# A planner that knows which neighbours cannot overlap, and a fixed table of seeds for its order

## The chip, the cores and the metric

The program runs on one core of one Trainium2 chip. Its time is the device time of one execution in microseconds, from the host's single launch to the end of the outputs; lower is better. Of each kernel several executions are timed, and one more is taken with the hardware profiler.

## What is computed

One inference step of a decoder trunk of two layers, for a prompt of 512 tokens and a group of 8 x 8 sample tokens, which share all weights (576 tokens together, 1024 channels, all in 32-bit floats).

```
h = rms_norm(x);  m = pooling mixer (layer 0) or gated DeltaNet mixer (layer 1)
x = x + rms_norm(m)
h = rms_norm(x);  f = (silu(h @ w_gate) * (h @ w_up)) @ w_out
x = x + rms_norm(f)
```

The pooling mixer takes trailing means over 2, 4, 8 and 16 positions, minus the token, and a linear map in each of four groups. The gated DeltaNet mixer projects h to q, k, v and z, runs a short causal convolution of width 4, and then a chunked delta rule over 16 value heads of 128 x 128: in each chunk a unit lower triangular matrix is inverted, and a state S is carried from chunk to chunk (the scan). Outputs are the tokens, the pooling rows, the convolution rows and the states.

## The kernel before

A matrix product in 32 bits is made of three TensorE products in the rounded type `fp32r`: every weight and every activation is split into a high part (`wh`, `hH`, `aH`; a ScalarE copy) and a low part (`wl`, `hL`, `aL`; the difference, on VectorE or GpSimd), and `mm3` multiplies high by high, high by low and low by high. The work comes in these stages: the pooling mixer, the first feed-forward (partly with Strassen's products), the DeltaNet mixer in four groups of four value heads, its output product, and the second feed-forward. In the DeltaNet mixer the group's own work (the *core*: decay matrices `QD`, the inverse built in `ii` and `Uw`, the small sample problem with `BD`, `TQ` and `ks`, then the scan with `vn`, `ve` and `S`, and the sample states `St`) is a chain in which TensorE, ScalarE and VectorE take turns, and the projections of the next group (`ps_m`, three products for each of eight blocks of rows) are there to fill TensorE in the meantime.

In what order each engine gets its instructions is not written in the code. The class `Plan` records every operation with the tiles that it reads and writes, gives each a cost (`cost`: a time `t`, and a hold `t` minus 85 ns on VectorE or minus 102 ns on ScalarE, since an instruction may start before its forerunner's end), and at `finish` lists them: `forward` goes through time, and each engine takes the operation of highest rank among those whose inputs are ready by these costs. Operations marked `EITHER` go to VectorE or GpSimd, whichever is taken first. The ranks are the latest starts that `backward` finds from an earlier list. On one engine the program then runs strictly in the order that stands in the list; between engines semaphores hold an instruction until its inputs are there, however long that takes on the chip. Where `forward` sees TensorE without work for more than 300 ns, `idle_until` puts small products of a matrix of ones into a free bank (`ps_w`, called fillers below), which keep the array busy and compute nothing.

After 40 rounds over the whole list, `refined` goes over the list in windows of 60 us in steps of 30 us. In each window it tries up to 40 random shifts of the ranks (one shift for all operations that write the same tile), and keeps the one whose worst lateness is least; 16 passes of this are made, and a pass is kept where the listed end comes earlier. Its costs take no account of the partition at which an operand starts, nor of the steps of a GpSimd copy.

Of the kernel before, what the change touches and what calls it, by code (L numbers as in the profile page):

```python
# [16 lines left out]
PSUM = bass.MemoryType.PSUM  # L17
# [39 lines left out]
class Plan:  # L57
# [8 lines left out]

    LAT = {"PE": 55.0, "ACT": 36.0, "DVE": 36.0, "POOL": 70.0, "SP": 60.0}
# [8 lines left out]
    PASSES, SPAN, STEP, TRIES, FEW = 16, 60000.0, 30000.0, 40, 6  # L76
# [83 lines left out]
    def cost(self, eng, method, out, ins, k):  # L160
# [24 lines left out]
        if eng == "POOL":  # L185
            if method in ("memset", "tensor_copy"):
                t = 0.85 * n + (100 if method == "memset" else 183)
            elif method == "affine_select":
                t = 1.1 * n + 190
            else:  # L190
                bc = any(list(x.ap)[-1][0] == 0 for x in ins if self.size(x) > 1)
                t = (1.75 if bc else 2.2) * n + 180
            return t - 60, t
        if method == "transpose":
            flat = all(list(x.ap)[-1][0] == 1 for x in ins + [out])
            t = 1.27 * n + 50 if flat else 1.95 * n + 80
        elif method == "scalar_tensor_tensor":
            t = 1.04 * n + 210
        elif method == "reciprocal":
            t = 6.2 * n + 153  # L200
        elif method in ("tensor_copy", "tensor_scalar") and not ps:
            t = 0.58 * n + 160
        else:
            t = 1.04 * n + 160
        return t - 85, t

    def put(self, method, calls, a, k):
# [39 lines left out]
        if "PE" in calls:  # L247
            rows, cols = self.rows(ins[0]), list(outs[0].ap)[0][1]
            mode = rows + (1000 if "tile_position" in k and cols < 128 else 0)
            work = self.size(outs[0]) / 2.4 * (1 if ins[0].dtype != F32 else 2 if method == "transpose" else 4)  # L250
            work *= rows * min(1.0, 0.25 * -(-cols // 32)) / 128
        elif method == "activation":
            mode = self.TABLE.get(str(a[2]).split(".")[-1], 0)
        cost = {e: self.cost(e, method, outs[0], ins, k) for e in calls}
        two = method in ("tensor_tensor", "scalar_tensor_tensor", "tensor_scalar", "tensor_copy") \
            and not any(x.space == PSUM for x in ins)
        self.ops.append((calls, cost, a, k, sorted(preds), mode, work, next(iter(calls)), two, method,
                         {x.tensor.name for x in ins + outs if x.space == PSUM}))
# [13 lines left out]
    def finish(self):  # L272
# [48 lines left out]
    def refined(self, plan, draw):  # L321

        late = self.backward(plan[1], plan[2])
        rank = [-t for t in late]
        order = sorted(range(len(late)), key=late.__getitem__)
        names = [self.name(o) for o in self.ops]
        done, state, a, first = ([], []), None, 0.0, 0

        def behind(found, b):

            nonlocal first
            log, times, taken, busy = found[-2], found[-1], found[2], 0.0
            worst = max((t - late[i] for (i, e), (t, _) in zip(log, times) if e is not None), default=-1e12)
            while first < len(order) and state is not None and state[2][order[first]]:
                first += 1
            k = first
            while k < len(order) and taken[order[k]]:
                k += 1
            return worst if k == len(order) else max(worst, b - late[order[k]])

        while True:
            b = a + self.SPAN
            best = None
            tries = self.TRIES
            k = 0
            while k < tries:
                trial = rank
                if k:
                    off, by = {}, draw.choice(self.STIR[2:])
                    trial = rank[:]  # L350
                    for i in window:
                        off.setdefault(names[i], by * (2.0 * draw.random() - 1.0))
                        trial[i] += off[names[i]]
                found = self.forward(trial, state, b, late, best and best[0])
                k += 1
                if found is None:
                    continue
                value = behind(found, b)
                if k == 1:
                    window = [i for i, e in found[-2] if e is not None]  # L360
                    work = sum(self.ops[i][1]["PE"][0] for i, e in found[-2] if e == "PE")
                    if work > 0.995 * self.SPAN:
                        tries = self.FEW
                if best is None or value < best[0]:
                    best = value, trial
            rank = best[1]
            found = self.forward(rank, state, a + self.STEP)
            done[0].extend(found[-2])
            done[1].extend(found[-1])
            state, a = found[:-2], a + self.STEP  # L370
            if not found[0]:
                return max(found[3].values()), *done

# [54 lines left out]
    def forward(self, rank, state=None, until=None, due=None, limit=None):  # L428
# [4 lines left out]
        if state is None:  # L433
# [13 lines left out]
            quiet = {}  # L447
        else:
            todo, left, taken, free, ready, avail, when, mode, dma, port, phases, fast, recent, busy, turn, still, \
                quiet = state  # L450
            left, taken, when, recent = left[:], taken[:], when[:], recent.copy()
            free, mode, port, turn, still, quiet = (dict(v) for v in (free, mode, port, turn, still, quiet))
# [54 lines left out]
        while todo:  # L507
# [40 lines left out]
            if limit is not None and t - due[i] >= limit:  # L548
                return None
            if mine is not q:  # L550
                q.remove((-rank[i], i))
                heapq.heapify(q)
# [39 lines left out]
        return (todo, left, taken, free, ready, avail, when, mode, dma, port, phases, fast, recent, busy, turn, still,  # L592
                quiet, order, times)

    def take(self, e, q, taken, mode):

        while taken[q[0][1]]:
            heapq.heappop(q)
        best = q[0]
        if self.ops[best[1]][5] not in (0, mode) and self.HOLD.get(e):  # L600
            same = min((x for x in q if not taken[x[1]] and self.ops[x[1]][5] in (0, mode)), default=None)
            if same is not None and same[0] - best[0] < self.HOLD[e]:
                best = same
        q.remove(best)
        heapq.heapify(q)
        return best[1]
# [1406 lines left out]
```

## Time and profile before

| | before |
|---|---|
| median of three executions | 1575.35 us |
| lowest and highest | 1569.87 and 1575.95 us |
| the profiled execution, its own time | 1574.86 us |
| its span, first to last instruction | 1573.1 us |
| TensorE (PE) busy | 1535.2 us, 98% |
| VectorE (DVE) busy | 1192.2 us, 76% |
| ScalarE (ACT) busy | 788.5 us, 50% |
| GpSimd (POOL) busy | 127.0 us, 8% |
| mean granted TensorE clock | 0.996 |

All numbers of the argument are of the profiled execution. A matmul's row lasts from its start until its result stands in PSUM, and the next ones start long before that; so the busy time of PE holds short stalls that the rows overlap, and only longer ones show as idle. A 32-bit product that is not split shows as two rows of the profile. Every recorded operation carries the line of the planner's call (L319 before), so groups are told apart by the tiles that they write and read. Names like `ps_k<-T,Uw` say: writes a PSUM tile `ps_k`, reads `T` and `Uw`; buffer numbers are left out in the profile, and `T` stands for the tile `T01`, `Rs` for `Rs2`, `R` for `R2`.

### The profile page before, as it was taken

The numbers are of one execution on the slowest core, as the hardware profiler recorded it, in microseconds if no ns is written. First come the engines' busy times: TensorE is split into PE (matmuls) and PEld (weight loads), VectorE is DVE, ScalarE is ACT, GpSimd is POOL, SyncE is SP. The second block draws the span as 40 slices with busy tenths as digits, with TensorE's granted clock in tenths as the row PEclk, the third lists the DMA queues.
The fourth block names the chain that finished last, engine by engine and source line by source line (L and its number), as shares of the span: only waits on it lengthen the run. The fifth ranks groups of instructions, "written<-read, shape, count | busy, mean of one in ns | idle before, by whom it ended". The sixth has DMA issues, their size and how long they took to land. (4 is left out here: it accounts for less than half of the span.)

```text
span 1573.1 us, 30432 instructions
## 1 busy us (share of the span) xinstructions
PE 1535.2 (98%) x11931; PEld 1471.2 (94%) x11931; DVE 1192.2 (76%) x2377; ACT 788.5 (50%) x1655; POOL 127.0 (8%) x257
## 2 busy tenths in 40 slices
PE   8999999999999999999999999999999999999997
PEld 8999999999999988898899889899999999999997
DVE  6894566677686898897998899668797485766855
ACT  7663443435556955453563553425465453434553
POOL 4110000000010021100220121000020000000000
PEclk9999999999999999999999999999999999999999
DMA  6464323232566332425243433655864432233253
GB/s 184 134 181 124 103 71 112 61 107 80 168 179 171 110 102 79 141 69 143 83 132 93 126 109 100 204 160 172 244 196 136 144 93 83 76 100 108 76 169 105
DMA packets 344902, 197.86 MB, mean 126 GB/s; under 512 B 13547, under 2 KB 337740, under 8 KB 344751
## 3 DMA queue, kind: packets, MB, share of 16 engines
q1 hardware_dynamic: 344759, 195.92, 43.0%
q8 instruction: 94, 1.54, 0.4%
q14 instruction: 49, 0.40, 0.1%
HBM read 165.60 MB, written 30.52 MB: 125 GB/s over the span
## 5 line engine op out<-in xcount | busy, mean ns | idle before, releaser
L319 ACT ACTIVATE wh<-wraw 128x1024 fp32r<-128x1024 f32 (+4 forms) x240 | 232.7, 975 | 215.0 <-PE ps_A L319 74.3
L319 DVE TENSOR_TENSOR wl<-wraw,wh 128x1024 fp32r<-128x1024 f32 (+4 forms) x232 | 257.3, 1115 | 66.5 <-ACT wh L319 49.4
L319 PE MATMUL ps_m<-hH,wh 128*128 128x256 f32 (+1 forms) x832 | 248.8, 311 | 2.1 <-ACT zz L319 1.5
L319 PE MATMUL ps_m<-hL,wh 128*128 128x256 f32 (+1 forms) x832 | 248.0, 309 | 0.0
L319 PE MATMUL ps_m<-hH,wl 128*128 128x320 f32 (+1 forms) x832 | 243.4, 307 | 0.0
L319 PEld LDWEIGHTS ps_m<-hH,wh 128*128 128x128 f32 x832 | 154.8, 189 | 7.4 <-ACT zz L319 2.7
L319 PEld LDWEIGHTS ps_m<-hL,wh 128*128 128x128 f32 x832 | 155.1, 189 | 3.2 <-issue 1.7
L319 PEld LDWEIGHTS ps_m<-hH,wl 128*128 128x128 f32 x832 | 153.7, 189 | 2.5 <-issue 0.8
L319 PE MATMUL ps_B<-hH,wh 128*128 128x320 f32 (+1 forms) x444 | 129.8, 305 | 0.2 <-DVE yo L319 0.2
L319 PE MATMUL ps_B<-hL,wh 128*128 128x320 f32 (+1 forms) x444 | 128.6, 304 | 0.0
L319 PE MATMUL ps_B<-hH,wl 128*128 128x320 f32 (+1 forms) x444 | 128.6, 304 | 0.0
L319 PE MATMUL ps_A<-hH,wh 128*128 128x256 f32 (+1 forms) x432 | 118.7, 290 | 0.5 <-DVE yo L319 0.5
L319 PE MATMUL ps_A<-hL,wh 128*128 128x256 f32 (+1 forms) x432 | 118.7, 292 | 0.1
L319 PE MATMUL ps_A<-hH,wl 128*128 128x256 f32 (+1 forms) x432 | 118.2, 292 | 0.0
L319 PE MATMUL ps_A<-aH,wh 128*128 128x288 f32 x352 | 99.3, 297 | 1.4 <-ACT wh L319 1.4
L319 PE MATMUL ps_A<-aL,wh 128*128 128x288 f32 x352 | 100.0, 295 | 0.0
L319 PE MATMUL ps_A<-aH,wl 128*128 128x288 f32 x352 | 99.7, 297 | 0.0
L319 PE MATMUL ps_B<-aH,wh 128*128 128x288 f32 x352 | 98.9, 297 | 0.5 <-DVE xa L319 0.5
L319 PE MATMUL ps_B<-aL,wh 128*128 128x288 f32 x352 | 98.6, 297 | 0.0
L319 PE MATMUL ps_B<-aH,wl 128*128 128x288 f32 x352 | 96.6, 296 | 0.0
L319 PEld LDWEIGHTS ps_B<-hH,wh 128*128 128x128 f32 x444 | 82.1, 188 | 1.0 <-issue 0.5
L319 PEld LDWEIGHTS ps_B<-hH,wl 128*128 128x128 f32 x444 | 81.9, 188 | 0.3 <-DVE wl L319 0.2
(467 smaller groups left out, 4063.8 us busy)
## 6 DMA issues: line engine op xcount, KB each, us to landing
wraw<-in_ffn_w_in_dram SPq DMA_DIRECT2D x77, 512.0 KB
wraw<-in_gdn_w_in_dram SPq DMA_DIRECT2D x56, 512.0 KB
graw<-in_ffn_w_in_dram SPq DMA_DIRECT2D x33, 512.0 KB
wraw<-in_ffn_w_out_dram SPq DMA_DIRECT2D x32, 448.0 KB
wraw<-in_gdn_w_out_dram SPq DMA_DIRECT2D x24, 512.0 KB
wraw<-in_ffn_w_out_dram SPq DMA_DIRECT2D x32, 320.0 KB
St<-in_state_gdn_rec_dram SPq DMA_DIRECT2D x32, 256.0 KB
out_dram<-St SPq DMA_DIRECT2D x32, 256.0 KB
```

The lines of the kernel that those rows point to most:

```text
L319: calls[e](*a, **k)
```

## The change

The instructions' work is the same; the planner that orders them is changed in three ways.

Its costs: after an instruction on VectorE or ScalarE whose operands start at a partition above 0, or before one, no overlap is counted, and 32 ns are added (`REBASE`, the flag `base`). A ScalarE instruction that reads what an earlier one on ScalarE wrote is ready 88 ns later (`SAME`). A copy on GpSimd with more than one free dimension costs 5.5 ns per element and 250 ns in place of 0.85 and 183; a VectorE `tensor_scalar` that reads PSUM costs 1.09 n + 200 in place of 1.04 n + 160; a small `scalar_tensor_tensor` from SBUF costs less. Costs are rounded to eighths of a nanosecond.

Its choice: an operation is taken by the least pair of rank and number in all cases, where before one of two paths kept a heap.

Its search: the 16 passes of random trials are replaced by five passes over a table, `CHOSEN`. For each window the table gives a list of seeds, and each seed shifts the ranks of all, a quarter or a sixteenth of the tiles in that window by up to 0.3, 1 or 3 us, drawn by a hash of the seed and the tile's number. Shifts add up, and nothing is compared.

```diff
+    SAME = {"ACT": 88.0}
+    REBASE = 32.0
...
-    PASSES, SPAN, STEP, TRIES, FEW = 16, 60000.0, 30000.0, 40, 6
+    SPAN, STEP = 60000.0, 30000.0
+    CHOSEN = (
+        "0: 34951 77998 29685 41485 12130 6250 58336 21398 12634 79632 3739 88189; 1: 90293 27366 58954 95454 "
...
         if eng == "POOL":
-            if method in ("memset", "tensor_copy"):
+            if method == "tensor_copy" and len(list(out.ap)) > 2:
+                t = 5.5 * n + 250
+            elif method in ("memset", "tensor_copy"):
                 t = 0.85 * n + (100 if method == "memset" else 183)
...
         elif method == "scalar_tensor_tensor":
-            t = 1.04 * n + 210
+            t = 1.04 * n + (210 if ps or n > 64 else 152)
+        elif method == "tensor_scalar" and ps:
+            t = 1.09 * n + 200
...
+        base = any(x.space != DRAM and x.offset >= list(x.ap)[0][0] for x in ins + outs)
...
-        for _ in range(self.PASSES):
-            found = self.refined(best, draw)
-            if found[0] < best[0]:
-                best = found
+        numbers = {}
+        self.number = [numbers.setdefault(self.name(o), len(numbers)) for o in ops]
+        for chosen in self.CHOSEN:
+            best = self.refined(best, chosen)
...
+            seeds = chosen.get(round(a / self.STEP), ())
+            if seeds:
+                window = [i for i, e in self.forward(rank, state, a + self.SPAN)[-2] if e is not None]
+                for seed in seeds:
+                    self.moved(rank, window, seed)
+            a += self.STEP
+            found = self.forward(rank, state, a)
...
+    def moved(self, rank, window, seed):
+
+        by, part, low = (300.0, 1000.0, 3000.0)[seed % 3], (1, 4, 16)[seed // 3 % 3], 0xffffffff
+        off = {}
+        for i in window:
+            k = self.number[i]
+            if k not in off:
...
+                off[k] = 0.0 if (y ^ y >> 15) % part else by * (2.0 * ((x ^ x >> 15) / 4294967296.0) - 1.0)
+            rank[i] += off[k]
...
+            elif e in past:
+                if past[e][1] or ops[i][11]:
+                    late = max(past[e][0] + self.REBASE - t, 0.0)
+                    hold, done = hold + late, done + late
+                past[e] = t + done, ops[i][11]
...
-                at = t + hold if to == e == "PE" else end + self.LAT[to]
+                at = t + hold if to == e == "PE" else end + self.LAT[to] + (self.SAME.get(e, 0.0) if to == e else 0.0)
```

What it moves is shown at three places. In the listings a name's number is the buffer, L319 and L447 are the line of the same call before and after.

The first is ScalarE in the fourth group's inversion, where the results of `ps_s` are turned into `T01` and `Uw` (the tile that the TensorE product `ps_k_2524` waits for). Before:

```order
L319 ACTIVATE Rs2_2515<-ps_k_2518 32x16x32 x2
L319 ACTIVATE hH_97<-og_2731 128x256
L319 ACTIVATE nco_2469<-ps_x_2468 27x512
L319 ACTIVATE hH_97<-og_2731 128x320
L319 ACTIVATE hH_97<-og_2732 128x256
L319 ACTIVATE hH_97<-og_2732 128x320
L319 ACTIVATE wh_2755<-wraw_2754 128x1024
L319 ACTIVATE hH_97<-og_2733 128x256
L319 ACTIVATE T01_2514<-ps_s_2522 32x8x32 x2
L319 ACTIVATE Uw_1209<-ps_s_2520 32x8x32 x2
```

and now:

```order
L447 ACTIVATE hH_97<-og_2735 128x320
L447 ACTIVATE Rs2_2515<-ps_k_2518 32x16x32 x2
L447 ACTIVATE ac_2736<-ps_m_2745 128x256
L447 ACTIVATE ac_2737<-ps_m_2747 128x256
L447 ACTIVATE T01_2514<-ps_s_2522 32x8x32 x2
L447 ACTIVATE Uw_1209<-ps_s_2520 32x8x32 x4
L447 ACTIVATE R2_2516<-ps_k_2524 64x512 x2
```

The high halves of `og` and the weight `wh_2755` stood between `Rs2` and `T01`, and now stand ahead of `Rs2` or behind the inversion. On TensorE, three `ps_m` products and four transposes stood between the last `ps_s_2520` and `ps_k_2524`; now it is 21 products `ps_m_2749` of 128x320.

The second is TensorE in the first group's sample problem, between the products of `qks` (whose results VectorE turns into `BD`) and the transposes of `BD`. Before:

```order
L319 MATMUL ps_k_1429<-qks_1214 64x128
L319 MATMUL ps_k_1429<-ident_68,qks_1214 64x128
L319 MATMUL ps_m_1382<-hL_98,wh_1379 128x256
L319 MATMUL ps_m_1382<-hH_97,wl_1380 128x256
L319 MATMUL ps_k_1432<-ident_68,BD_1210 128x128
L319 MATMUL ps_m_1382<-hH_97,wh_1379 128x256
```

and now, from the last four of the filling products on:

```order
L447 MATMUL ps_m_1629<-hL_98,wh_1624 128x320
L447 MATMUL ps_m_1629<-hH_97,wl_1625 128x320
L447 MATMUL ps_m_1629<-hH_97,wh_1624 128x320
L447 MATMUL ps_m_1629<-hL_98,wh_1624 128x320
L447 MATMUL ps_m_1629<-hH_97,wl_1625 128x320
L447 MATMUL ps_k_1432<-ident_68,BD_1210 128x128
L447 MATMUL ps_m_1629<-hH_97,wh_1624 128x320
L447 MATMUL ps_k_1432<-ident_68,BD_1210 128x128
```

Between the last `qks` product and the first transpose of `BD` stood two products; now 19 products (four of 128x256, 15 of 128x320) and a transpose stand there.

The third is TensorE in the second group's inversion, from the products `ps_s_1810` and `ps_s_1808` to `ps_k_1812`, which waits for `T01`, made of `ps_s_1810`. Before, the end of the two products and what follows:

```order
L319 MATMUL ps_s_1810<-Rs2_1803,Uw_1209 64x32 x4
L319 MATMUL ps_s_1808<-Uw_1209,Rs2_1803 64x64 x6
L319 MATMUL ps_m_2017<-hH_97,wh_2014 128x256
L319 MATMUL ps_m_2017<-hL_98,wh_2014 128x256
L319 MATMUL ps_m_2017<-hH_97,wl_2015 128x256
L319 MATMUL ps_m_2017<-hH_97,wh_2014 128x256
L319 MATMUL ps_m_2017<-hL_98,wh_2014 128x256
L319 MATMUL ps_k_1812<-T01_1802,Uw_1209 64x64 x16
```

and now:

```order
L447 MATMUL ps_s_1810<-Rs2_1803,Uw_1209 64x32 x16
L447 MATMUL ps_s_1808<-Uw_1209,Rs2_1803 64x64 x16
L447 MATMUL ps_m_2017<-hH_97,wl_2015 128x256
L447 MATMUL ps_m_2017<-hH_97,wh_2014 128x256
L447 MATMUL ps_m_2017<-hL_98,wh_2014 128x256
L447 MATMUL ps_m_2017<-hH_97,wl_2015 128x256
L447 MATMUL ps_m_2017<-hH_97,wh_2014 128x256
L447 MATMUL ps_m_2017<-hL_98,wh_2014 128x256
L447 MATMUL ps_k_1812<-T01_1802,Uw_1209 64x64 x16
```

The two products were mixed, so that the last of `ps_s_1810` came six before the end; now all of it comes first, and one more filling product follows.

Over the whole program the number of fillers goes from 57 to 41. Of the `ve` products of the scan (`ve<-vn,kde`), 28 were on VectorE and 4 on GpSimd; now 20 and 12. The VectorE program has 2360 instructions in place of 2377.

More of the change, by code (lines that the diff above doesn't have):

```diff
@@ L319, in finish @@
                 calls[e](*a, **k)
[L321 to L339, printed above, removed]
-        while True:
[L342 to L367, printed above, removed]
@@ new lines, in refined @@
+    def refined(self, plan, chosen):
+        rank = [-t for t in self.backward(plan[1], plan[2])]
+        done, state, a = ([], []), None, 0.0
+        chosen = {int(w): [int(x) for x in seeds.split()] for w, seeds in (p.split(":") for p in chosen.split(";"))}
+        while True:
+            seeds = chosen.get(round(a / self.STEP), ())
[5 more added lines that the diff above has]
+            found = self.forward(rank, state, a)
@@ L368, in refined @@
             done[0].extend(found[-2])
             done[1].extend(found[-1])
-            state, a = found[:-2], a + self.STEP
+            state = found[:-2]
             if not found[0]:
                 return max(found[3].values()), *done
+    def moved(self, rank, window, seed):
[4 more added lines that the diff above has]
+            if k not in off:
+                y = k * 0x9e3779b1 + seed * 0xc2b2ae35 & low
+                y = (y ^ y >> 13) * 0x27d4eb2f & low
+                x = seed * 0x9e3779b1 + k * 0x85ebca6b & low
+                x = (x ^ x >> 15) * 0x2c1b3c6d & low
+                x = (x ^ x >> 12) * 0x297a2d39 & low
+                off[k] = 0.0 if (y ^ y >> 15) % part else by * (2.0 * ((x ^ x >> 15) / 4294967296.0) - 1.0)
+            rank[i] += off[k]
@@ L426, in backward, with forward @@
         return late
-    def forward(self, rank, state=None, until=None, due=None, limit=None):
+    def forward(self, rank, state=None, until=None):
         ops, succ = self.ops, self.succ
@@ L447, in forward @@
             quiet = {}
+            past = {"DVE": (0.0, False), "ACT": (0.0, False)}
         else:
             todo, left, taken, free, ready, avail, when, mode, dma, port, phases, fast, recent, busy, turn, still, \
-                quiet = state
+                quiet, past = state
             left, taken, when, recent = left[:], taken[:], when[:], recent.copy()
-            free, mode, port, turn, still, quiet = (dict(v) for v in (free, mode, port, turn, still, quiet))
+            free, mode, port, turn, still, quiet, past = (dict(v) for v in (free, mode, port, turn, still, quiet, past))
             ready = {e: v[:] for e, v in ready.items()}
@@ L547, in forward @@
             i = self.take(e, mine, taken, mode.get(e))
[L548 to L552, printed above, removed]
+            q.remove((-rank[i], i))
+            heapq.heapify(q)
             hold, done = ops[i][1][e]
@@ L592, in forward @@
         return (todo, left, taken, free, ready, avail, when, mode, dma, port, phases, fast, recent, busy, turn, still,
-                quiet, order, times)
+                quiet, past, order, times)
     def take(self, e, q, taken, mode):
-        while taken[q[0][1]]:
-            heapq.heappop(q)
-        best = q[0]
+        q = [x for x in q if not taken[x[1]]]
+        best = min(q)
         if self.ops[best[1]][5] not in (0, mode) and self.HOLD.get(e):
-            same = min((x for x in q if not taken[x[1]] and self.ops[x[1]][5] in (0, mode)), default=None)
+            same = min((x for x in q if self.ops[x[1]][5] in (0, mode)), default=None)
             if same is not None and same[0] - best[0] < self.HOLD[e]:
                 best = same
-        q.remove(best)
-        heapq.heapify(q)
         return best[1]
```

7 lines of the change are left out of this document (4 added, 3 removed), and 118 rows, old and new, of the table CHOSEN.

## The prediction

> **What bounds the kernel now.** I read the page's shares first, then the windows by stage, then the list of what TensorE waited for, and last the rows around the longest waits.
>
> ```profile
> PE 1535.2 (98%) x11931; PEld 1471.2 (94%) x11931; DVE 1192.2 (76%) x2377; ACT 788.5 (50%) x1655; POOL 127.0 (8%) x257
> ```
>
> TensorE is busy for 1535.2 of the 1573.1 us, so 37.9 us show as idle, and this is the stock an order can draw on, with the fillers and with stalls too short to show. The matmuls themselves are the same before and after (fillers apart). The windows say where the stock lies (columns: the stretch and its length, busy time and instructions of PE, of the weight loads, of DVE, ACT and POOL, the granted clock, the DMA share, GB/s).
>
> ```profile
> 0.00:40.00 40.00, 35.21 (x235) 32.78 (x236) 28.07 (x74) 29.29 (x70) 18.05 (x77) 0.91 0.67 181
> 240.00:400.00 160.00, 160.00 (x1203) 159.55 (x1203) 116.45 (x185) 70.03 (x103) 0.00 (x0) 1.00 0.31 90
> 520.00:1080.00 560.00, 540.13 (x4525) 492.10 (x4524) 481.34 (x1148) 278.23 (x788) 74.90 (x140) 1.00 0.42 120
> 760.00:840.00 80.00, 77.62 (x572) 71.20 (x571) 78.12 (x191) 44.64 (x140) 18.56 (x34) 1.00 0.37 104
> 1400.00:1500.00 100.00, 100.00 (x755) 99.89 (x754) 72.36 (x112) 44.25 (x65) 0.00 (x0) 1.00 0.30 86
> 1500.00:1540.00 40.00, 36.30 (x275) 34.67 (x274) 25.48 (x41) 21.20 (x36) 0.00 (x0) 1.00 0.68 200
> 1540.00:1573.00 33.00, 25.34 (x187) 23.60 (x186) 15.31 (x27) 12.96 (x26) 0.00 (x0) 0.95 0.25 79
> ```
>
> The feed-forwards (240 to 400, 1400 to 1500) have no idle at all: nothing can be won there by order, and a worse order could only lose. The first 40 us have 4.8 us idle, the last 73 us 11.4 us. The DeltaNet stretch from 520 to 1080 has 560 - 540.13 = 19.9 us, and there VectorE works 481.34 of 560 us, from 760 to 840 even 78.12 of 80. So this stretch is a race between TensorE and VectorE, run in strict order on both. What TensorE waited for, over the whole program (us in total, times, longest):
>
> ```profile
> PE ps_x L319 <- DVE vt L319: 3.0, 4, 1.4
> PE ps_x L319 <- DVE vs L319: 2.4, 4, 0.9
> PE ps_k L319 <- issue: 2.2, 1, 2.2
> PE ps_k L319 <- DVE TQ L319: 2.0, 2, 1.1
> PE ps_A L319 <- DVE xst L319: 1.8, 1, 1.8
> PE ps_k L319 <- DVE QD L319: 1.8, 3, 1.0
> ...
> PE ps_B L319 <- ACT nh L319: 1.4, 2, 1.2
> PE ps_A L319 <- ACT wh L319: 1.4, 1, 1.4
> PE ps_k L319 <- DVE Uw L319: 1.3, 4, 0.7
> ```
>
> Many small waits, mostly on VectorE, none over 2.2 us. That looks like a plan whose costs were a little short.
>
> **The change, part by part.**
>
> *The costs.* The rows around 567 us show the thing that the planner now prices.
>
> ```profile
> 566.35 0.29 DVE L319 SCALAR_TENSOR_TENSOR BD<-ps_k,bet,des 64x64 f32<-64x64 f32 x1
> 566.68 0.21 DVE L319 TENSOR_TENSOR ii<-ii 128x30 f32<-128x30 f32 x1
> 566.92 0.22 DVE L319 TENSOR_TENSOR TQ<-ps_k,des 64x64 f32<-64x64 f32 x1
> 567.17 0.22 DVE L319 TENSOR_TENSOR ii<-ia,ii 128x58 f32<-128x58 f32 x1
> 567.42 0.23 DVE L319 TENSOR_TENSOR TQ<-ps_k,des 64x64 f32<-64x64 f32 x1
> 567.70 0.33 PE L319 MATMUL ps_k<-ident,BD 128*128 128x128 f32 x1 [1.09 <-DVE TQ L319]
> ...
> 571.03 0.83 DVE L319 SCALAR_TENSOR_TENSOR ac<-u,cwt,ac 128x600 f32<-128x600 f32 x1
> 571.78 0.23 DVE L319 TENSOR_TENSOR ii<-ia,ii 128x78 f32<-128x78 f32 x1
> ```
>
> `ii` at 571.78 starts 0.08 us before `ac` ends (571.03 + 0.83 = 571.86). The `TQ` at 566.92 ends at 567.14 and the next row starts at 567.17, 0.03 later; so beside a half-tile instruction a pair takes 0.11 us more. The old costs counted the overlap everywhere, and VectorE fell behind its list wherever such pairs are dense; here TensorE paid 1.09 us for it. The Trainium skill (VectorE: DVE Perf Modes, section on two Vector instructions with no wait between them) states that an instruction is held when its inputs or output start in another quadrant than those of the instruction before, which these rows agree with; by it two neighbours that both start in the same upper quadrant are not held, so the planner's rule would be a little too careful there, which costs no more than a few unneeded tenths of cover.
>
> At this place the order gives 20 instructions of cover where two stood. Their pace is read from the chain of waits:
>
> ```profile
> 1196.67 19.40 PE ps_B L319 x132
> 1098.09 12.00 PE ps_A L319 x97
> ```
>
> 19.40 / 132 is 0.147 us for a product of 320 columns, 12.00 / 97 is 0.124 for a stretch of mostly 256. Cover goes from 2 x 0.124 = 0.25 us to 15 x 0.147 + 4 x 0.124 + 0.1 = 2.8 us. The wait of 1.09 us is inside the 2.6 us that come to it, so it goes, and so, most likely, does the second one on `TQ` (2.0 together). I take **-2.0 us**, between -2.0 and 0.
>
> *The fourth inversion.*
>
> ```profile
> 997.26 0.78 ACT L319 ACTIVATE hH<-og 128x256 fp32r<-128x256 f32 x2 [0.83 <-DMA og<-og_d]
> 997.95 1.04 ACT L319 ACTIVATE wh<-wraw 128x1024 fp32r<-128x1024 f32 x1
> 998.89 0.40 ACT L319 ACTIVATE hH<-og 128x256 fp32r<-128x256 f32 x1
> 999.32 0.77 ACT L319 ACTIVATE T<-ps_s 32x256 f32<-32x256 f32 x2
> 1000.58 0.30 PE L319 MATMUL ps_k<-T,Uw 128*64 128x64 f32 x2 [2.24 <-issue]
> ```
>
> TensorE stood still for 2.24 us ("issue" here hides ScalarE's late `T`), since ScalarE split activations and a weight first, behind a transfer of `og`. In the new order none of these stands between, and 21 x 0.147 = 3.1 us of products cover the wait. I take **-2.2 us**, bounds -2.24 and 0.
>
> *The other inversions.* All of `ps_s_1810` first starts ScalarE's `T01` earlier, and one more product (0.12 us) follows. The `DVE Uw` row (1.3) is the wait this can touch; I take **-0.8 us**, bounds -1.3 and +0.5.
>
> *The rest of the DeltaNet stretch.* Of 19.9 us idle, 19.9 - 2.24 - 2.0 - 1.3 = 14.4 remain, spread over `vt`, `vs`, `QD` and others. Better costs and another search can shorten them or make others; without a row for it I bound the term by 0 and by half of this stock, and take a quarter, **-3.6 us**. Stalls that do not show as idle lie in the same stretch: the weight loads are busy all the time in a full stage (159.55 of 160) and only 492.10 of 560 here. Part of these 68 us is due to 32-bit products, which take longer than their weights; I count a twentieth, **-3.4 us**, bounds 0 and -10.
>
> *Fillers.* 57 before, 41 now.
>
> ```profile
> L315 PE MATMUL ps_w<-ones x114: 270/275/582, 1.3 to 1536.7; 128*128 128x128 f32 x114
> ```
>
> 114 rows for 57 fillers. At the pace above, 0.124 us a row, one costs some 0.25 us (an estimate), and 16 fewer are 4.0 us, if what they covered is no longer a wait. I take **-2.5 us**, bounds -4.0 and 0.
>
> *What is moved to GpSimd.* Eight `ve` more:
>
> ```profile
> L319 DVE TENSOR_TENSOR ve<-vn,kde x28: 410/416/468, 617.3 to 1069.9; 128x256 f32<-128x256 f32 x28
> L319 POOL TENSOR_TENSOR ve<-vn,kde x4: 615/932/1522, 632.4 to 896.5; 128x256 f32<-128x256 f32 x4
> ```
>
> Each takes VectorE 0.42 us less and delays the scan's `ps_s<-ve,kt` by 0.93 - 0.42 = 0.52 us, 4.1 us in all if nothing covers it; queued behind it on TensorE is the next projection product. Most have more than 1.5 us of products in between, so I take **+1.0 us**, bounds 0 and +4.1.
>
> *Start and end.* The wait on `xst` (1.8) and those on `nh` (1.4) and the weight (1.4) have the same neighbours in both orders: 0, cover none, bounds -2 and +2.
>
> Sum: -2.0 - 2.2 - 0.8 - 3.6 - 3.4 - 2.5 + 1.0 = -13.5. The profiled execution took 1574.86 us, 1.8 more than its span and 0.5 below the median of the three runs, 1575.35. 1574.86 - 13.5 gives **1561.4 us**, 0.9% less.
>
> **The rivals.**
>
> *VectorE sets the pace (no change).* If VectorE's work is the limit from 520 to 1080, cover on TensorE only moves waits. For it: 78.12 of 80 us. Against: the whole stretch leaves 560 - 481.34 = 78.7 us free. Then only the 17 instructions that leave VectorE count, at 0.42 us some 7 us in a stretch where it is 86% busy, and about half of it reaches the end: 1571 us.
>
> *GpSimd blocks VectorE (slower).* One `ve` on GpSimd took 1.522 us instead of 0.615. If both engines hold each other up, each of the 12 costs the scan up to 1.522 - 0.416 = 1.1 us, and VectorE as much. It decides from the point where a `ve` lands later than its cover, some 1.4 us at the tightest. 8 x 1.1 = 8.8 us above, with none of the gains but the fourth inversion's: 1574.9 + 8.8 - 2.2 = 1581.5. Against: the list of waits above names no tile of GpSimd. The Trainium skill (SBUF — State Buffer, section "SBUF: two separate sides") states that VectorE and GpSimd share a port pair that one of them holds for a whole instruction while the other is blocked; the spread from 615 to 1522 ns agrees with it.
>
> *The search finds much more (faster still).* If half of the 14.4 us and 10 us of unseen stalls go, and all fillers count: -2.0 - 2.2 - 1.3 - 7.2 - 10 - 4.0 = -26.7, 1548 us.
>
> That the change does nothing is out: thousands of rows of the order differ.
>
> **How the numbers follow.** Forecast (about -8 to -20 us) 0.47; much more 0.20; no change 0.21; slower 0.12. The measurement tells a change from none at about 0.5%, 7.9 us, so faster is below 1567.5: nearly all of the first two cases, 0.65; within 0.5%: the no-change case and the forecast's upper edge, 0.24; slower 0.11. The range from 1545 to 1577 leaves out the far part of "much more" and most of "slower". The likeliest case alone has 1555 to 1567.
>
> **What would show it.** Right: PE idle from 520 to 1080 falls from 19.9 to about 12 us; no 2.2 us row before `ps_k<-T,Uw`; no `TQ` among the waits; 82 rows of `ps_w`. Wrong: the same idle under other names (VectorE's pace), or `ps_s` waiting for POOL `ve`, with means over 1 us. The forecast fails if new waits in the feed-forwards appear, which have none now, or if the plan's costs still fall short of the chip elsewhere.

## The result, and the profile after

| | before | the change |
|---|---|---|
| median, executions of the same chip | 1573.22 us, 4 | 1549.95 us, 4 |
| lowest and highest | 1569.87 to 1575.95 | 1548.15 to 1552.44 |
| ratio, 95% interval | 1 | 0.9854, 0.9827 to 0.9881 |
| profiled execution, own time and span | 1574.86 and 1573.1 us | 1548.15 and 1546.4 us |
| mean granted TensorE clock in it | 0.996 | 0.994 |

The change makes the kernel 1.5% faster: 23 us by the medians, 26.7 us between the two profiled executions. The forecast was faster by 13.5 us. The sign is right and the time lies inside the range, but below the 1555 to 1567 us of the likeliest case; the gain is 1.7 times the predicted one by the medians, and twice between the profiled executions. So the question of the experiments is where the second half came from. Two of the runs below had one execution far longer than their others (4553.53 us with the new costs and the old search, 1630.37 us with all `ve` on VectorE), and their medians and ratios are of the other executions.

The busy times of the changed kernel (first part of the page):

```profile
PE 1522.8 (98%) x11899; PEld 1466.0 (95%) x11899; DVE 1181.3 (76%) x2360; ACT 791.1 (51%) x1655; POOL 130.4 (8%) x274
```

TensorE's idle time is now 1546.4 - 1522.8 = 23.6 us; it was 37.9. So 14.3 of the 26.7 us are idle time that is gone. The other 12.4 us were "busy" time before: rows that end later because they were issued late, and fillers. Next the windows of the changed kernel, with the columns of the prediction:

```profile
0.00:40.00 40.00, 35.43 (x230) 32.13 (x230) 24.02 (x67) 29.35 (x70) 16.39 (x75) 0.91 0.66 181
40.00:80.00 40.00, 39.79 (x289) 38.14 (x289) 36.80 (x93) 29.06 (x63) 6.79 (x10) 0.91 0.49 146
240.00:400.00 160.00, 159.81 (x1199) 158.92 (x1198) 115.31 (x185) 69.90 (x103) 0.00 (x0) 1.00 0.31 89
520.00:1080.00 560.00, 551.37 (x4684) 510.16 (x4683) 491.05 (x1153) 291.18 (x806) 87.32 (x162) 1.00 0.45 129
760.00:840.00 80.00, 79.33 (x591) 73.87 (x591) 78.05 (x198) 41.21 (x124) 16.64 (x35) 1.00 0.36 103
```

From 520 to 1080 us the idle time is 560 - 551.37 = 8.6 us, where 19.9 stood and about 12 were expected. In the same 560 us TensorE now finishes 4684 rows instead of 4525, but the window now also holds some 22 us more of the stage behind the scans, since these end earlier. From 760 to 840 us VectorE is as full as before (78.05 of 80, it was 78.12), and yet TensorE's idle time fell from 2.38 to 0.67 us. The feed-forwards (240 to 400) are as full as they were, within 0.2 us.

Where along the program the time went can be read from one tile. `ve` is written once or twice in every step of the scan, from the first group to the last. Rows of the changed kernel (count, least, median and largest duration in ns, then the first and the last start):

```profile
L447 DVE TENSOR_TENSOR ve<-vn,kde x20: 406/421/426, 614.8 to 1047.7; 128x256 f32<-128x256 f32 x20
L447 POOL TENSOR_TENSOR ve<-vn,kde x12: 612/614/1268, 626.3 to 901.1; 128x256 f32<-128x256 f32 x12
```

The first `ve` started at 617.3 us before and starts at 614.8 now; the last one at 1069.9 and now at 1047.7. So 2.5 us were won up to the first scan, 452.6 - 432.9 = 19.7 us between the first and the last `ve`, and the remaining 4.5 of the 26.7 us behind them. The DeltaNet stretch carries the gain. The windows between the first and the last `ve`, before and now, hold nearly the same work:

```profile
617.30:1069.90 452.60, 436.78 (x3642) 395.77 (x3640) 388.47 (x917) 211.11 (x621) 62.95 (x121) 1.00 0.41 119
614.80:1047.70 432.90, 425.59 (x3619) 390.35 (x3618) 378.30 (x897) 207.73 (x614) 76.03 (x138) 1.00 0.44 126
```

TensorE's idle time falls there from 15.8 to 7.3 us, which is 8.5 of the 19.7 us. The other 11.2 us are busy time, with only 23 rows fewer; the time in which no weights are loaded falls by 14.3 us (from 56.8 to 42.6). So more was won than the idle time shows. The list of what TensorE waited for, now:

```profile
PE ps_x L447 <- DVE vt L447: 3.1, 3, 2.2
PE ps_A L447 <- DVE xst L447: 1.6, 1, 1.6
PE ps_w L443 <- POOL ones L224: 1.3, 1, 1.3
PE ps_k L447 <- DVE QD L447: 0.9, 2, 0.7
PE ps_k L447 <- DVE T L447: 0.8, 1, 0.8
...
PE ps_k L447 <- issue: 0.4, 1, 0.4
...
PE ps_s L447 <- POOL ve L447: 0.2, 1, 0.2
```

`TQ` and `vs` are gone from the list, and `nh` before `ps_B` (1.4 us) and the 2.24 us of "issue" have left its top. `vt` is as long as it was (3.0 before).

### The profile page after: what moved, and what is told of

Its sections match the earlier page's. It is cut to its first block, busy times and chain, and to the rows that moved or that the text cites. A ratio compares the mean times of both kernels' runs of the same rounds, so it can differ in the third digit from the quotient of the medians.

```text
span 1546.4 us, 30413 instructions
## 1 busy us (share of the span) xinstructions
PE 1522.8 (98%) x11899; PEld 1466.0 (95%) x11899; DVE 1181.3 (76%) x2360; ACT 791.1 (51%) x1655; POOL 130.4 (8%) x274
## 4 chain that ended last, share of the span: by engine, by line
PE 85%; DVE 10%; DMA 2%; issue 1%; ACT 1%; POOL 0%; DVEq 0%; SPq 0%; ACTq 0%; POOLq 0%
PE ps_B L447 28%; PE ps_A L447 26%; PE ps_m L447 17%; PE ps_s L447 5%; PE ps_k L447 4%; PE ps_x L447 2%; PE ps_n L447 1%; PE ps_e L447 1%; DVE wl L447 1%; DVE Uw L447 1%; DVE ii L447 1%; DVE ac L447 1%; DMA vt<-z_d 1%; PE ps_g L447 1%; DMA QD<-gc_d 0%
## 5 line engine op out<-in xcount | busy, mean ns | idle before, releaser
L447 ACT ACTIVATE wh<-wraw 128x1024 fp32r<-128x1024 f32 (+4 forms) x240 | 233.4, 976 | 223.1 <-PE ps_A L447 79.5
L447 DVE TENSOR_TENSOR wl<-wraw,wh 128x1024 fp32r<-128x1024 f32 (+4 forms) x232 | 257.9, 1117 | 78.2 <-ACT wh L447 49.8
L447 PE MATMUL ps_m<-hH,wh 128*128 128x320 f32 (+1 forms) x832 | 249.5, 312 | 0.5 <-ACT u L447 0.3
L447 PE MATMUL ps_m<-hL,wh 128*128 128x320 f32 (+1 forms) x832 | 245.1, 306 | 0.3 <-DVE hL L447 0.3
L447 PE MATMUL ps_m<-hH,wl 128*128 128x320 f32 (+1 forms) x832 | 241.2, 305 | 0.0
L447 PEld LDWEIGHTS ps_m<-hH,wh 128*128 128x128 f32 x832 | 154.3, 189 | 5.6 <-issue 1.1
L447 PEld LDWEIGHTS ps_m<-hL,wh 128*128 128x128 f32 x832 | 154.5, 189 | 3.0 <-issue 0.6
L447 PEld LDWEIGHTS ps_m<-hH,wl 128*128 128x128 f32 x832 | 153.3, 189 | 2.0 <-issue 0.8
L447 PE MATMUL ps_B<-hH,wh 128*128 128x320 f32 (+1 forms) x444 | 128.3, 305 | 0.1
L447 PE MATMUL ps_B<-hH,wl 128*128 128x320 f32 (+1 forms) x444 | 127.9, 304 | 0.0
L447 PE MATMUL ps_B<-hL,wh 128*128 128x320 f32 (+1 forms) x444 | 127.5, 303 | 0.0
L447 PE MATMUL ps_A<-hL,wh 128*128 128x256 f32 (+1 forms) x432 | 120.4, 291 | 0.0
L447 PE MATMUL ps_A<-hH,wh 128*128 128x256 f32 (+1 forms) x432 | 119.7, 292 | 0.0
L447 PE MATMUL ps_A<-hH,wl 128*128 128x256 f32 (+1 forms) x432 | 119.1, 290 | 0.0
L447 PE MATMUL ps_B<-aH,wh 128*128 128x288 f32 x352 | 99.7, 298 | 0.2 <-DVE xa L447 0.2
L447 PE MATMUL ps_A<-aH,wl 128*128 128x288 f32 x352 | 99.3, 295 | 0.0
L447 PE MATMUL ps_A<-aH,wh 128*128 128x288 f32 x352 | 98.8, 297 | 0.2 <-DVE y L447 0.2
L447 PE MATMUL ps_B<-aL,wh 128*128 128x288 f32 x352 | 98.5, 297 | 0.0
L447 PE MATMUL ps_A<-aL,wh 128*128 128x288 f32 x352 | 97.9, 295 | 0.0
L447 PE MATMUL ps_B<-aH,wl 128*128 128x288 f32 x352 | 97.8, 296 | 0.0
L447 PEld LDWEIGHTS ps_B<-hH,wh 128*128 128x128 f32 x444 | 81.5, 188 | 1.3 <-ACT wh L447 0.5
L447 PEld LDWEIGHTS ps_B<-hH,wl 128*128 128x128 f32 x444 | 81.8, 188 | 0.1
```

The costliest lines, as they stand in the source:

```text
L447: calls[e](*a, **k)
```

## The experiments

Theory A says that the costs made the gain: with prices that hold on the chip, the list holds on the chip. Theory B says that the search made it: the table holds seeds that were picked, by much more trying than the old passes did. In what follows every ratio is against the kernel before, measured together with the run, with its 95% interval. What is called the new costs below contains the new choice and the rounding as well; these two were not tried alone.

### Costs and search apart

The new costs with the old search (16 passes of random trials, 2 as the draw's start). The edit is shown in part, against the changed kernel; `refined` is the one of before again:

```diff
+    PASSES, TRIES, FEW = 16, 40, 6
...
-        for chosen in self.CHOSEN:
-            best = self.refined(best, chosen)
+        for _ in range(self.PASSES):
+            found = self.refined(best, draw)
+            if found[0] < best[0]:
+                best = found
```

> The change's costs (no overlap beside partition offsets, the 88 ns, the GpSimd copies) with the 16 passes of random trials of before in place of the table. Theory A, the costs: most of the gain of 23 to 26 us is here, since the list is no longer ahead of the chip: 1550 to 1558 us. Theory B, the search: the costs alone give little, the table gives the rest: 1566 to 1575 us. If both have a part: about 1560 to 1564 us. PE idle from 520 to 1080 us, 19.9 us before and 8.6 us after the change, would be under 11 by A and over 15 by B.

1569.42 us, ratio 0.9977 (0.9961 to 0.9994), as theory B expected. The window of the DeltaNet stretch:

```profile
520.00:1080.00 560.00, 547.97 (x4598) 503.01 (x4598) 484.87 (x1147) 293.25 (x805) 82.65 (x149) 0.99 0.42 121
```

Idle is 12.0 us there, close to what the forecast wanted and between the bounds of the two theories (11 and 15), and the whole program still gained only 3.6 us by the ratio. Then both costs without any search after the 40 rounds: the new ones with an empty table, and the kernel before with its passes set to zero.

```diff
-    CHOSEN = (
-        "0: 34951 77998 ...",
-        ...
-    )
+    CHOSEN = ()
```

> The change with an empty table: its costs and only the 40 rounds over the whole list. By A (costs) at or below the kernel before, 1565 to 1575 us; by B (search) clearly above before, 1585 to 1610 us, since windows were always searched.

1587.93 us, ratio 1.0089 (1.0058 to 1.0121).

```diff
-    PASSES, SPAN, STEP, TRIES, FEW = 16, 60000.0, 30000.0, 40, 6
+    PASSES, SPAN, STEP, TRIES, FEW = 0, 60000.0, 30000.0, 40, 6
```

> The kernel before without its 16 passes, costs as they were. Against the run with the new costs and an empty table it shows the costs alone where neither searches windows. By A it is slower than that run by 10 us or more, by B within 5 us of it; both expect it above before, 1585 to 1610 us.

1594.19 us, ratio 1.0119 (1.0090 to 1.0148). Without a search the new costs are worth 1.0089 - 1.0119 = -0.3%, with overlapping intervals. That is 4.7 us, within the 5 us of theory B (6.3 us by the medians, which lies between the two theories), and both kernels are above the one before, as expected. To see how much one list differs from another by luck, the kernel before and the kernel of the first run were each made once more from another draw:

```diff
-    ROUNDS, STIR, SEED = 40, (0.0, 0.0, 300.0, 1000.0, 3000.0), 2
+    ROUNDS, STIR, SEED = 40, (0.0, 0.0, 300.0, 1000.0, 3000.0), 3
```

> The kernel before with the seed of its random trials 3 in place of 2, nothing else: another list of the same planner. Theory C, the luck of one list: the lists of one planner differ by 10 us or more, and the gain of the change is partly that, 1555 to 1590 us. By A and B the lists of one planner lie within 5 us: 1568 to 1579 us.

1567.56 us, ratio 0.9956 (0.9940 to 0.9972), for the old costs: 6 to 7 us, more than the 5 us that A and B allow and less than the 10 us of theory C.

> The new costs with the old random trials, drawn from 3 instead of 2. The new costs with draw 2 gave 1570.0 us, the old costs with draw 2 give 1573.4 and with draw 3 1567.6. Theory L (the costs alone are worth less than the luck of one draw): 1562 to 1577 us, and the mean of the two draws with new costs lies within 4 us of the mean of the two with old costs, 1570.5. Rival C (the costs are worth something by themselves): below 1562, so that the mean of the new ones lies 4 us or more under that of the old ones.

1566.26 us, ratio 0.9935 (0.9915 to 0.9955), for the new costs. Set side by side:

| after the 40 rounds | old costs | new costs | difference |
|---|---|---|---|
| nothing | 1.0119 | 1.0089 | -0.0030 |
| 16 random passes, draw 2 | 1 | 0.9977 | -0.0023 |
| 16 random passes, draw 3 | 0.9956 | 0.9935 | -0.0021 |
| the five passes of the table | (below) | 0.9854 | |

The costs are worth 0.2 to 0.3%, 3 to 5 us, each time. No pair proves it, since the luck of a draw is 0.4% (0.9956 against 1, 0.9935 against 0.9977); the three pairs agree, but three are few against a luck that is larger than the difference. In the last run's text the bound between its two readings was 4 us for the means of two draws; they differ by (1 + 0.9956 - 0.9977 - 0.9935) / 2 = 0.22%, 3.5 us, so the reading that luck is larger than the costs holds, and the costs' own share is small, if it is there at all. The remaining 0.8 to 1.2% (0.9935 or 0.9977 to 0.9854) is the search on the new costs. Theory B carries most of the change. What an equally long search would find on the old costs was not tried, so how much of these 0.8 to 1.2% needs the new costs stays open.

### Does it matter which seeds are in the table?

The table with every seed moved on by a constant, so that there are as many shifts of the same sizes, but not the picked ones:

```diff
-                    self.moved(rank, window, seed)
+                    self.moved(rank, window, seed + 99999)
```

> The change with 99999 added to every seed of its table: as many shifts, of the same sizes and shares of tiles, in the same windows, but other draws. Theory B1, the seeds were picked and it is the picking that counts: other draws shift without aim, 1600 us or more, above the 1588 us of the empty table. Theory B2, it is the kind of shift and the re-listing that help, whichever the draw: 1545 to 1565 us.

1612.54 us, ratio 1.0240 (1.0215 to 1.0264): 2.4% slower than before, and 1.5% slower than no shifts at all. Its window:

```profile
520.00:1080.00 560.00, 533.73 (x4380) 485.52 (x4380) 466.44 (x1114) 283.26 (x767) 64.90 (x132) 0.97 0.40 113
```

26.3 us idle, and 304 rows fewer than in the change's window. A part of the loss is clock: the mean granted clock of its executions is 0.983, and 0.988 with the empty table, 0.005 x 1610 = 8 of the 24.6 us between the two (an estimate). The table itself with the old costs (`SAME` empty, no `base` flag, and the old prices):

```diff
-    SAME = {"ACT": 88.0}
+    SAME = {}
...
-            if method == "tensor_copy" and len(list(out.ap)) > 2:
-                t = 5.5 * n + 250
-            elif method in ("memset", "tensor_copy"):
+            if method in ("memset", "tensor_copy"):
...
-            t = 1.04 * n + (210 if ps or n > 64 else 152)
-        elif method == "tensor_scalar" and ps:
-            t = 1.09 * n + 200
+            t = 1.04 * n + 210
...
-        base = any(x.space != DRAM and x.offset >= list(x.ap)[0][0] for x in ins + outs)
+        base = False
```

> The change's table with the costs of before (no held neighbours, no 88 ns, cheap GpSimd copies; the rounding stays). If the seeds fit only the list that the new costs make, they shift without aim here: 1590 us or more. If a seed is good by itself and the costs hardly matter: within 8 us of the change, 1550 to 1558 us.

1626.26 us, ratio 1.0331 (1.0306 to 1.0356). So the seeds are no description of good places in the program. They fit one list: on the list that other costs give, the same shifts act like noise, 3.3% slower than before and 2.1% slower than the old costs with no shifts at all (1.0119). How the seeds were picked is not on record; that they were picked follows from the two runs.

### How much of the table is needed?

```diff
-        for chosen in self.CHOSEN:
+        for chosen in self.CHOSEN[:1]:
```

> The changed kernel with the new costs and only the first of the table's five passes of seeds. New costs with no pass stand at 1587.9 us, with all five at 1550, so the passes are worth 38 us together. Theory S (each pass is a further step of one search, the first ones worth most): the first pass alone gives a third to two thirds of it, 1563 to 1576 us, and TensorE's idle time from 520 to 1080 us lies between that of the two. Rival W (the seeds only work as a whole, as when they were all shifted or put on the list of the old costs): 1585 us or more.

1556.76 us, ratio 0.9879 (0.9853 to 0.9906). The windows of the run with the empty table, and of this one:

```profile
520.00:1080.00 560.00, 543.51 (x4544) 497.19 (x4543) 481.05 (x1132) 290.54 (x788) 74.54 (x148) 0.99 0.42 119
520.00:1080.00 560.00, 549.95 (x4638) 504.61 (x4638) 491.12 (x1167) 296.06 (x817) 78.55 (x148) 1.00 0.44 125
```

The idle time, 16.5 us with the empty table, is 10.0 us here and 8.6 us with all five passes, in the order that theory S expected.

With `CHOSEN[:3]` in the same place:

> As the run before, with the first three of the five passes. Theory S: another step on the way, 1553 to 1563 us, clearly below the first pass alone and 3 to 13 us above the whole table. Rival W: 1575 us or more, with nearly all of the gain in the last passes.

1557.03 us, ratio 0.9879 (0.9860 to 0.9897). The first pass takes the ratio from 1.0089 to 0.9879, which is 89% of the way to 0.9854. That is more than the two thirds that were expected at most, and 1556.76 us lies below the 1563 of the text above. Passes two and three added nothing that can be measured, where theory S expected another step, and the last two 0.25%, with overlapping intervals. The rival that the passes only work together is refuted. Pass one alone beats both 16-pass random searches (0.9935, 0.9977). What a pass of the table has and a random pass has not is that many shifts add up in one window (the first pass lists 30 seeds for one of its windows), while a random pass keeps one shift per window at most. Whether this or the picking itself makes the difference was not tried apart.

### The places that the prediction named

In the changed kernel's own list, the products that cover three waits were moved behind the waiting instruction: 16 of them at the first group's `BD` (`ps_k_1432`), 20 at the second group's `BD` (`ps_k_1793`), 18 at the fourth inversion (`ps_k_2524`). The numbers in the diff are the products to be left in front (at the first place the timeline shows four); `bare`, which does the moving, is left out here:

```diff
+        listed = self.bare(best[1])
...
-            for i, e in best[1]:
+            for i, e in listed:
...
+    BARE = {"ps_k_1432": 2, "ps_k_1793": 9, "ps_k_2524": 3}
```

> The change's list with the cover at three places put back to about what it was: 16 products behind the BD transposes of the first group, 20 behind those of the second, 18 behind the product that waits for T in the fourth group's inversion, each moved to just after the waiting product. Nothing else moves. If the cover is what removed the waits, they come back there: 1.1 + 0.9 + 2.2 us by the profile of before, 3 to 5 us in all. If ScalarE and VectorE are now early at these places anyway, the waits stay under 0.3 us each and the time within 1 us.

1554.5 us, ratio 0.9874 (0.9854 to 0.9895); against the change's 0.9854 that is +0.2%, 3 us, and 4.5 us by the medians, with overlapping intervals, so only the rows can tell. From the list of TensorE's waits in this run:

```profile
PE ps_x L448 <- DVE vt L448: 5.0, 4, 2.3
PE ps_k L448 <- DVE BD L448: 2.5, 2, 2.0
```

TensorE waits for `vt` 1.9 us longer than in the change (3.1), although none of the three places waits for `vt`; so not all of the difference need be due to the cover. From the timeline, the longer of the two waits on `BD`:

```profile
566.81 0.33 PE L448 MATMUL ps_k<-ident,BD 128*128 128x128 f32 x1 [1.98 <-DVE BD L448]
```

And the windows of 5 us around that place:

```profile
565.00:570.00 5.00, 3.19 (x16) 3.19 (x17) 4.25 (x14) 1.93 (x4) 0.00 (x0) 0.81 0.28 88
570.00:575.00 5.00, 5.00 (x35) 5.00 (x35) 2.08 (x6) 0.98 (x4) 0.00 (x0) 0.85 0.01 1
```

A wait on `BD` is back, now of 1.98 us where 1.09 stood before, and in its two windows of 5 us the granted clock is 0.81 and 0.85: 0.19 x 5 + 0.15 x 5 = 1.7 us of full clock are lost on top. The cover at this place is worth some 2 to 4 us. At the second group's `BD` 0.5 us came back, where 0.9 stood before. So the two `BD` places give 2.5 us of wait for the 2.0 of the first term. At the fourth inversion it is different. ScalarE and TensorE in the same run:

```profile
992.07 0.76 ACT L448 ACTIVATE T<-ps_s 32x256 f32<-32x256 f32 x2 [0.41 <-PE ps_s L448]
...
993.30 0.31 PE L448 MATMUL ps_m<-hH,wl 128*128 128x320 f32 x1
993.54 1.46 PE L448 MATMUL ps_k<-T,Uw 128*64 128x64 f32 x32
```

With only three products in front, `ps_k<-T,Uw` starts 0.24 us behind the last of them and shows no wait, because `T` is done at 992.83 already. In the kernel before three products (and four transposes) stood there, and TensorE waited 2.24 us. So what took that wait away is ScalarE's order, in which no `hH` of `og` and no weight stands in front of `T`. The cover of 21 products adds little: in the changed kernel the same 32 products take 1.15 us instead of 1.46, so taking 18 of them away cost some 0.3 us.

```profile
990.25 1.15 PE L447 MATMUL ps_k<-T,Uw 128*64 128x64 f32 x32
```

Together 2.5 us of wait came back, less than the 3 to 5 us of the text above.

### GpSimd's `ve`, and the fillers

All 12 `ve` of the changed list given to VectorE, at the same place of the list:

```diff
+                if e == "POOL" and "DVE" in calls and self.name(ops[i]).startswith("ve"):
+                    e = "DVE"
```

> The change's list with the 12 ve products that it puts on GpSimd put on VectorE, at the same place in the list. If GpSimd delays the scan: 1 to 4 us faster. If VectorE is what lacks time there: 12 x 0.42 = 5 us of VectorE more, 0 to 4 us slower.

1549.1 us, ratio 0.9846 (0.9815 to 0.9877): no difference from the change (0.9854) that shows, with an interval of 0.3%, 5 us, to either side. The longest GpSimd `ve` of the changed kernel took 1.268 us and TensorE waited 0.2 us in all for one of them; neither engine holds the other up at a price that can be measured.

The same list with its 41 fillers left out:

```diff
                 if e is None:
-                    self.tc.nc.tensor.matmul(self.banks[i[0]][i[1]][0][:, :self.idle.shape[1]], self.idle, self.idle,
-                                             start=True, stop=True)
                     continue
```

> The changed kernel's own list with all 41 fillers (products whose result nobody reads, on ps_w) left out. The prediction gave a filler 0.25 us. Theory F1 (they stand where TensorE would wait anyway): 1547 to 1553 us, no difference to be measured from the changed kernel. F2 (they cost what they take): 41 times 0.25 is 10 us, so 1538 to 1543. F3 (they hold the granted clock up): the clock from 0 to 80 us falls below the 0.91 of the changed kernel, or it falls after the last waits, and the time is 1555 us or more.

1548.74 us, ratio 0.9836 (0.9803 to 0.9869): no difference either (F1); the 10 us of F2 would be a ratio of 0.979, outside the interval. What TensorE waited for up to 80 us shows why, in the changed kernel and in this run:

```profile
PE ps_A L447 <- POOL bm L447: 0.4, 1, 0.4
PE ps_A L445 <- POOL bm L445: 4.6, 1, 4.6
```

The fillers stand in time that TensorE would wait through; what they take is not won by leaving them out. The 1555 us of F3 did not come; on the granted clock itself the runs decide nothing. In this run's profiled execution (the slowest of its four, 1557.41 us) it was 1.00 in the first 20 us and 0.76 in the next, and 0.83 and 1.00 in the changed kernel's; but the run with all `ve` on VectorE has the same fillers as the changed kernel and 1.00 in both windows:

```profile
0.00:20.00 20.00, 13.24 (x79) 11.79 (x80) 13.09 (x43) 14.74 (x33) 13.31 (x73) 1.00 0.83 246
20.00:40.00 20.00, 18.49 (x112) 17.26 (x110) 9.09 (x20) 12.93 (x34) 2.40 (x1) 0.76 0.49 115
```

So one profile each cannot tell what the fillers do to the clock.

## Why the prediction was right or wrong

**What bounds the kernel** was read rightly: the gain lies in the stretch from 520 to 1080 us, the feed-forwards stayed full, and no new waits appeared there.

**The range held in part by luck.** It reaches from 1545 to 1577 us because it leaves room for the rival "The search finds much more"; the likeliest case alone, 1555 to 1567 us, missed.

The sum, term by term, against the profiled executions (26.7 us):

| group of terms | predicted | by the two profiles |
|---|---|---|
| idle: `BD` place, fourth inversion, other inversions, rest of the stretch (and the ends) | -2.0 - 2.2 - 0.8 - 3.6 = -8.6 | -14.3 |
| stalls that do not show as idle | -3.4 | -8.4 |
| fillers | -2.5 | -4.0 (an estimate) |
| `ve` on GpSimd | +1.0 | none that shows |
| sum | -13.5 | -26.7 |

The fillers are 32 rows fewer (114 before), at the prediction's estimate of 0.124 us a row:

```profile
L443 PE MATMUL ps_w<-ones x82: 270/275/581, 1.3 to 1509.9; 128*128 128x128 f32 x82
```

The stalls are what is left of the 12.4 us of busy time, so the sum closes by construction. The clock is in no term: 0.994 instead of 0.996 is some 3 us against the change (an estimate).

**The named places were right, and about of the right size.** The waits on `TQ` and the 2.24 us before `ps_k<-T,Uw` are gone, and taking the cover away brings 2.5 us back at the two `BD` places. One reason in it was wrong: at the fourth inversion the cover was counted as half of the cure, and the run without it shows that ScalarE's order does nearly all of it. For the other inversions (-0.8) the row `DVE Uw` (1.3 us) is gone from the list; no run takes that place alone.

**The mis-sized terms are the two that had no row:** the rest of the stretch ("took a quarter" of 14.4 us) and the unseen stalls ("a twentieth" of 68 us). They were sized as what better costs would bring. The idle time of the stretch fell by 11.3 us, of which 5.0 were the named places' predicted share; so the rest gave some 6 us instead of 3.6, and 3.0 us of idle time went outside the stretch. The stalls gave 8.4 instead of 3.4. The runs show why: the step that failed is the one that read the waits as "a plan whose costs were a little short". Costs alone bring at most 3 to 5 us of some 23; the rest needs the table's search, which the terms of the forecast mention in two words ("another search") and size by no row of their own; only a rival has it in its name. It could have been seen from the diff that a window of the table has up to 30 shifts where a random pass kept one.

**The fillers** were a term of their own and should not have been. They are another form of the planned wait: leaving all 41 out changes nothing that can be measured, so the 4.0 us that went with 16 of them most likely belong to the waits that the new list no longer has.

**The `ve` term** was +1.0 within 0 to 4.1. The run shows no difference, but its interval of 5 us is wider than these bounds.

**Start and end**, taken as 0: 2.5 us were won up to the first `ve`, although the clock from 40 to 80 us was 0.91 where the kernel before had 0.96:

```profile
40.00:80.00 40.00, 39.95 (x297) 38.08 (x296) 33.79 (x82) 27.47 (x59) 6.63 (x7) 0.96 0.46 136
```

That is 0.05 x 40 = 2.0 us of clock lost. An estimate of the order's own gain there is thus 4 to 5 us. The wait on `xst` stayed (1.6 us, 1.8 before), as was said; that on `nh` before `ps_B` shrank from 1.4 to 0.4 us.

**The rivals.** That VectorE sets the pace, so that cover only moves waits, is refuted by the 23 us and in the window that spoke for it: with 78.05 of 80 us of VectorE, TensorE's idle time is 0.67 us. VectorE can still be a limit in this window, where TensorE's weight loads are busy for 73.87 of 80 us only; no run tried it. That GpSimd blocks VectorE, at 1581.5 us, is refuted by the time and by the run with all `ve` on VectorE. "The search finds much more", at 1548 us, had the right mechanism in its name and the right time; that its sum, -26.7, equals the measured difference to a tenth is chance, since its terms were bounds and not sizes. It got 0.20 where the likeliest case got 0.47, because the profile of before was asked how long its waits are, and cannot say how far a better order can go.

## What to carry to other kernels

Where a plan in strict order is the limit, ask first how good the search behind it is: build the list once more from another draw. Here that alone moved the time by 0.4%, more than the corrected costs did, and it says that the list is not the best. A table of picked shifts belongs to the list that it was made for; with the old costs under it the kernel was 3.3% slower than before and 2.1% slower than with no table, so such a table is made again when the costs change. And a wait that shows on one engine can be cured on another: look at what stands in front of the late instruction on its own engine before adding cover to the one that waits.

## What the runs showed of the hardware

**A wait of about 2 us on TensorE can cost more than itself.** In the run with three passes the timeline has one such wait:

```profile
723.20 0.30 PE L447 MATMUL ps_k<-T,Uw 128*64 128x32 f32 x2 [2.25 <-DVE Uw L447]
```

and the windows of 5 us around it:

```profile
720.00:725.00 5.00, 2.75 (x37) 2.25 (x38) 4.88 (x7) 0.38 (x1) 0.66 (x1) 1.00 0.29 86
725.00:730.00 5.00, 5.00 (x74) 4.60 (x73) 1.90 (x3) 1.18 (x2) 0.81 (x2) 0.51 0.61 171
730.00:735.00 5.00, 5.00 (x61) 4.27 (x59) 0.75 (x1) 3.12 (x7) 0.00 (x0) 0.50 0.33 94
735.00:740.00 5.00, 5.00 (x70) 4.35 (x66) 2.61 (x4) 1.76 (x5) 0.00 (x0) 0.62 0.54 157
740.00:745.00 5.00, 5.00 (x37) 4.41 (x34) 2.66 (x6) 1.97 (x6) 0.00 (x0) 1.00 0.93 247
```

After 2.25 us without work the granted clock is half for some 14 us, (0.49 + 0.50 + 0.38) x 5 = 6.9 us of full clock. It does not follow each time. The changed kernel's longest wait in the stretch is as long, and no lower clock follows; its timeline and its windows:

```profile
857.70 0.66 PE L447 MATMUL ps_x<-ident,vt 128*128 128x128 f32 x4 [2.23 <-DVE vt L447]
```

```profile
855.00:860.00 5.00, 2.77 (x46) 2.31 (x44) 1.88 (x2) 1.22 (x3) 0.00 (x0) 1.00 0.62 160
860.00:865.00 5.00, 5.00 (x33) 4.23 (x34) 2.66 (x6) 2.29 (x5) 0.00 (x0) 1.00 0.69 203
```

In the run with the cover taken away the same product waits 2.31 us for `vt`, and there the clock does fall, for 0.33 x 5 = 1.7 us of full clock:

```profile
860.00:865.00 5.00, 3.04 (x30) 2.82 (x32) 1.88 (x2) 0.58 (x1) 0.00 (x0) 0.67 0.50 139
```

The Trainium skill (TensorE: Matmul & The Clock Gate, Part 1: The HAM clock gate) states that the clock is halved after an idle window of about 3.4 us, and that the windows run freely and do not start with the work. The half clock agrees with these rows, the length does not: 1.98, 2.25 and 2.31 us of wait were enough here, and 2.23 us was not. What decides between them, the window's phase or the short gaps around the wait, was not tried.

**The longest wait that is left in the stretch is for a transfer.** The timeline of the changed kernel has `vt` on VectorE, for which TensorE waits those 2.23 us, and the issue of its reload on SP's queue:

```profile
851.34 0.53 SPq L447 DMA_DIRECT2D vt<-z_d  x1
...
856.89 0.75 DVE L447 SCALAR_TENSOR_TENSOR vt<-ps_x,prm,vt 128x512 f32<-128x512 f32 x1 [5.33 <-DMA vt<-z_d]
```

The plan's price for such a reload, 2000 + 65536 x 4 / 240 ns, is 3.1 us; here 856.89 - 851.34 = 5.55 us went by from its issue to the instruction that was waiting for it. A weight load of 512 KB was issued 0.48 us ahead of it on the same queue; whether the reload was held up behind it is not shown. The changed costs do not touch this price, and `vt` heads TensorE's list of waits before (3.0 us) and after (3.1 us). Whether a larger price would shorten it, after a new search, was not tried.
